# Low halves of the last down weights by VectorE, and loads that stand behind the last pair

## The chip, the cores and the metric

The kernel runs on one core of a Trainium2 chip. TensorE multiplies, VectorE and ScalarE do the element work, GpSimd does a share of it and issues some transfers, SyncE issues the others. What counts is the device time of the core in microseconds, as the median of repeated runs. Beside it there is one profiled execution, from which every view below is taken.

## The reference, cut to what matters

One inference step of a two-layer decoder on 520 rows: 512 of a prompt and 8 single decode rows, model width 1024. Layer 0 mixes tokens with windowed attention, layer 1 with gated linear attention (GLA). After the mixer each layer has a normalisation and this feed-forward part:

```python
def conv_ffn(x, buf, w_up, conv_w, conv_b, w_down):
    h = x @ w_up                                   # 1024 -> 2 x 2816
    a, u = h[..., :D_FF], h[..., D_FF:]
    ap = jnp.concatenate([buf, a], axis=1)
    c = conv_b + sum(conv_w[j] * ap[:, j:j + T] for j in range(3))
    return (gelu(c) * u) @ w_down, ap[:, T:]       # 2816 -> 1024

x = layer_norm(ALPHA * x + sublayer(x))            # after the mixer and after conv_ffn
```

All is float32. The kernel keeps that accuracy by splitting every operand into a high and a low part of the matmul type fp32r.

## The kernel before, in words

**Products.** Channels lie on partitions, rows of tokens on the free axis, in two groups: a (256 rows) and b (264). Each product of a 128x128 weight block takes three matmuls: high x high, high weight x low data, low weight x high data. A weight unit is one `128x1024` tile, 512 KB, that is eight such blocks. `product` (L219 to L241) does a whole unit for one group into one PSUM bank (`accp`); with `behind` set (L225) it does the low weight parts in a second pass (L238), not block by block (L235).

**Loading a unit** (`load_unit`, L176 to L196). SyncE fetches the raw weights into one of two buffers (`RAWS = 2`, L184), ScalarE rounds them to the high part `wh` (L189). The low part `wl` = raw - wh is made in one of two ways: by a subtraction on VectorE (L195), or by `low_by_dma` (L198 to L201), where ScalarE writes -wh into `wl` (L200) and a transfer from GpSimd's queue adds the raw weights to it from memory, on the way (L201). There are six slots of `wh`/`wl`. `load_next` starts the load of the next unit when a slot is free; `release` frees one, so a load is set off at the place in the program where a unit is finished. A scheduler then fixes the order of the instructions on each engine ahead of time; each engine works through its own queue strictly in that order. `issue_after(x)` keeps what is written inside it behind x.

**The feed-forward part.** 22 column blocks of the hidden layer. The first four go one by one, the other 18 as `ffn_pair` (L809 to L880): gate and value weights together, by seven half products of sums of blocks (a11, a12, s1 to s4, a22; L303 to L305 in `half_product`), merged by VectorE additions (`merged`, `conv`, L828), then the convolution (L860 to L863), gelu (L866), the product with the value branch (L867) and the split into high and low hidden values (`hs_a` and `hh_b` by ScalarE at L308, `hs_a` and `hl_b` by VectorE at L309). A pair takes four loads (`pair_tasks`): three "live" slots and one "half" slot. Down products of hidden blocks 0 to 13 run between the pairs (`ffn_down2`). Pairs are named here by their column block: pair 20 and pair 21 are the last two.

**The last down units.** Blocks 14 to 21 go into eight units, here d0 to d7, one per 128 output channels (`ffn_down`, L915 to L932). Four of them are begun ahead for group a (`HEADS = 4`, `down_steps`, L904 to L913) with the seven blocks that are ready before pair 21 is done: d0 and d1 with their low parts, d2 and d3 without. These four heads fill all four `accp` banks (`ACCS = 4`). After each unit and group comes a step of the normalisation (`ln_chunk`): VectorE adds the product to x (L330), which frees the bank, then squares (ScalarE, L350) and sums (L362, L363) follow; `ln_end` closes it (L366 to L441), and writes the next layer's inputs `xs_a`, `xh_b`, `xl_b` (L433 to L435). Group a runs four units ahead of group b.

**Row sums** (`row_sums`, L449 to L491) work out sums of rows of weights and inputs for the pairs' shortcut, in portions; `yield n` says after how many products the next portion may come.

The functions that the diff touches stand below with their lines.

Of the kernel before, what the change touches and what calls it, by code (L numbers as in the profile page):

```python
# [22 lines left out]
KD = 8  # L23
# [6 lines left out]
NF = 22  # L30
# [33 lines left out]
LOWS = 7  # L64
# [17 lines left out]
def parted(rows):  # L82

    return rows.rearrange("p (j t) -> p t j", t=2)


def in_turn(rows):

    return rows.rearrange("p t j -> p j t")
# [10 lines left out]
class Net:  # L100
# [70 lines left out]
    def wide(self):  # L171
        return self.acc.tile([P, 2, 512], F32, name="widep")


    def load_unit(self, u, pieces=1, late=False):
        src, nt = self.units[u][0], self.units[u][1]  # L176
        nc = self.nc
        if nt == 0:
            return self.load_rank(u)
        r = self.raw.tile([P, KD * P], F32, name="raw")  # L180
        h, l = ((self.wx if u == self.extra else self.wts).tile([P, KD * P], F32R, name=name) for name in ("wh", "wl"))
        n = nt * P // pieces
        for c in (slice(i * n, (i + 1) * n) for i in range(pieces)):
            nc.sync.dma_start(out=r[:, c], in_=src[:, c])  # L184
            if late:
                self.spawn(self.parts(u, h[:, c], l[:, c], r[:, c], src[:, c]), 1)
                continue
            if u >= HIACT:
                nc.scalar.activation(h[:, c], r[:, c], AF.Copy)  # L189
            else:  # L190
                nc.gpsimd.tensor_scalar(h[:, c], r[:, c], 1.0, 0.0, op0=ALU.mult, op1=ALU.add)
            if self.units[u][2] in (self.ffn_down2, self.ffn_down, self.ffn_gate, self.ffn_value):
                self.low_by_dma(l[:, c], h[:, c], src[:, c])
            else:
                nc.vector.tensor_tensor(l[:, c], r[:, c], h[:, c].bitcast(F32), op=ALU.subtract)  # L195
        self.w[u] = (h, l)  # L196
# [22 lines left out]
    def product(self, g, u, rh, rl):  # L219
        nc = self.nc  # L220
        h, l = self.w[u]
        nt = self.units[u][1]

        tail = u in self.phases[2::3] or g.i and u in self.phases[2:4]
        behind = g.i == 0 and nt == KD and not tail and any(e < u < e + LOWS for e in (*self.phases[2:4], *self.phases[5:6]))  # L225
        ps = self.acc.tile([P, 512], F32, name="accp")
        o = ps[:, :g.n].rearrange("p (j t) -> p j t", t=2)
        for k in range(nt):
            ks = slice(k * P, (k + 1) * P)
            xh, xl = in_turn(rh[:, k]), in_turn(rl[:, k])  # L230
            nc.tensor.matmul(o, h[:, ks], xh, start=k == 0, stop=False)  # L231
            if not tail:
                nc.tensor.matmul(o, h[:, ks], xl, start=False, stop=False)  # L233
            if not behind:
                nc.tensor.matmul(o, l[:, ks], xh, start=False, stop=not tail and k == nt - 1)  # L235
        for k in range(nt) if tail or behind else ():
            w, r = (h, rl) if tail else (l, rh)
            nc.tensor.matmul(o, w[:, k * P:(k + 1) * P], in_turn(r[:, k]), start=False, stop=k == nt - 1)  # L238
        self.final = self.nc.cur_bb.bb.instructions[-1]
        return ps[:, :g.n]  # L240
# [210 lines left out]
    def row_sums(self, i):  # L451


        nc, half, n = self.nc, KD // 2, P
        a, b = self.groups
        hi, lo = slice(half, KD), slice(0, half)
        v = nc.vector
        bias = lambda m: self.par[:, C_LNB + i * KD + m:C_LNB + i * KD + m + 1]
        step = self.pp.tile([P, half], F32, name="step")
        p0 = C_LNB + i * KD  # L460
        nc.gpsimd.tensor_tensor(step, self.par[:, p0 + half:p0 + KD], self.par[:, p0:p0 + half], op=ALU.subtract)
        wide = lambda t: t.rearrange("p (k c) -> p k c", k=half)
        even = lambda t: t.rearrange("p k (j t) -> p k t j", t=2)
        row = lambda g, k: g.x[:, k, 0:256]
        self.t1 = [self.ln.tile([P, NT - 256], F32, name=name, bufs=c)[:, :256] for name, c in (("sq", 2), ("sq", 2), ("mu", 1), ("msq", 1))]
        with self.tc.issue_after(self.rest):
            v.tensor_tensor(self.t1[0], row(a, 0), row(b, 0), op=ALU.subtract)
        for k in range(1, half):
            v.tensor_tensor(self.t1[k], row(a, k), row(b, k), op=ALU.subtract)
        yield 1  # L470
        ts = self.pp.tile([P, 2, half, NS], F32, name="tsum")
        gap = step.unsqueeze(2).broadcast_to([P, half, NS])
        for q, x, y, op in ((0, lo, hi, ALU.subtract), (1, hi, lo, ALU.add)):
            v.tensor_tensor(ts[:, q], b.x[:, x, 256:], b.x[:, y, 256:], op=ALU.subtract)
            v.tensor_tensor(ts[:, q], ts[:, q], gap, op=op)
            self.split(self.th[q][:, :, :, n:], self.tl[q][:, :, :, n:], even(ts[:, q]))
        r = wide(self.pp.tile([P, KD * P], F32, name="raw", bufs=2))
        for k in range(half):
            v.scalar_tensor_tensor(r[:, k], row(b, half + k), bias(half + k), self.t1[k], op0=ALU.add, op1=ALU.add)
        th, tl = self.th[0][:, :, :, :n], self.tl[0][:, :, :, :n]  # L480
        nc.scalar.activation(th, even(r), AF.Copy, scale=-1.0)
        for k in range(half):
            v.scalar_tensor_tensor(tl[:, k], even(r)[:, k], -1.0, th[:, k].bitcast(F32), op0=ALU.mult, op1=ALU.subtract)
        yield 2
        for k in range(half):
            v.scalar_tensor_tensor(r[:, k], r[:, k], bias(half + k), row(a, half + k), op0=ALU.subtract, op1=ALU.subtract)
        self.split(self.th[2], self.tl[2], even(r))
        yield 2
        for k in range(half):
            v.scalar_tensor_tensor(r[:, k], row(b, half + k), step[:, k:k + 1], row(b, k), op0=ALU.add, op1=ALU.subtract)  # L490
        self.split(self.th[1][:, :, :, :n], self.tl[1][:, :, :, :n], even(r))  # L491
# [316 lines left out]
    def ffn_pair(self, u, layer, j, q):  # L808


        nc, W = self.nc, self.w[u]
        a, b = self.groups
        if j == PAIRED:
            self.row_sum1()
            self.close(self.cp_cm)
            self.cp, self.cp_cm = self.open(f"merged{layer}")
            self.m = [self.cp.tile([P, 2, 2 + NT], F32, name=f"merged{i}") for i in range(2)]
            self.c = [self.cp.tile([P, 2, NT - 256], F32, name=f"conv{i}") for i in range(2)]
            for t in self.m:
                nc.gpsimd.memset(t[:, 0, 0:2], 0.0)  # L820
            self.close_psum()
            self.open_wide()
        half = KD // 2
        part = lambda g, ks: (g.xh[:, ks], g.xl[:, ks])
        lo, hi = slice(0, half), slice(half, KD)
# [5 lines left out]
        g, h = M[:, 0], M[:, 1, 2:]  # L831
# [19 lines left out]
        self.half_product(p[:, 0], W["s4"], part(b, hi), m)  # L851
        self.release()
        self.half_product(p[:, 1], W["s3"], t3, m)
        self.half -= 1
        self.load_next()
        add(M[:, :, 2 + n:], p[:, :, :m], both(C[:, 0]))
        add(h[:, :n], p[:, 1, :n], C[:, 1, :n])
        w, cb = self.taps(layer, j)
# [9 lines left out]
        self.split(a.hh[:, q], a.hl[:, q], parted(h[:, :n]))  # L868
        self.split(b.hh[:, q], b.hl[:, q], parted(h[:, n:]))
        if j == NF - 1:  # L870
            nc.scalar.dma_start(out=self.O["conv_p"][layer], in_=self.nconv_p)
            nc.scalar.dma_start(out=self.O["conv_s"][layer], in_=self.nconv_s)
            for cm in (self.cp_cm, self.pp_cm, self.fp_cm):
                self.close(cm)
            self.close_psum()
            self.open_acc()
# [420 lines left out]
            self.todo.pop(0)  # L1297
            f()

    def release(self):  # L1300
        self.live -= 1
        self.load_next()

    def run(self):
        nc = self.nc
        self.plan()
        self.nu = self.live = WSLOTS
        self.todo, self.half, self.more, self.extra = [], 0, False, None
        self.attn_open()
        self.later, self.slot, self.seq, self.norm = [], 0, 0, None  # L1310
        for i, u in self.order():
# [144 lines left out]
```

## Time and profile before

| what | value |
|---|---|
| median of three runs | 1129.21 us (1127.98 to 1132.0) |
| the profiled execution | 1128.26 us |
| span in its profile | 1126.5 us, mean granted TensorE clock 0.989 |
| TensorE busy | 1072.6 us, 95% |
| VectorE, ScalarE, GpSimd busy | 872.6, 664.6, 335.7 us |
| last down units of layer 0, of layer 1 | about 463 to 521 us, 1060 to 1113 us of the span |

The page lists busy time by engine and the costliest groups of instructions; the view of waits says, per engine and line, what the engine stood waiting for (total, times, longest); the timeline lists instructions with start, length and, in brackets, the idle time ahead of them and what ended it; a table of stretches gives busy time, granted clock (PEclk), share of the transfer engines and GB/s of each stretch.

### The profile page before, as it was taken

How to read it: one execution, taken by the hardware profiler on the slowest of the kernel's cores; microseconds unless marked ns; L12 is line 12 of the kernel's file. 1: busy time of each engine (PE TensorE's matmuls, PEld its weight loads, DVE VectorE, ACT ScalarE, POOL GpSimd, SP SyncE). 2: the span in 40 equal slices, each digit the busy share in tenths (PEclk: the TensorE clock that was granted, in tenths of full speed). 3: DMA queues.
4: the chain of work that ended last, by engine and by line, in shares of the span. 5: the costliest groups of instructions: out<-in, count | busy, mean ns of one | idle time of the engine just before them, and what ended most of it. 6: DMA issues, size and time to landing. Idle time of an engine off the chain costs nothing.

```text
span 1126.5 us, 23813 instructions
## 1 busy us (share of the span) xinstructions
PE 1072.6 (95%) x9174; PEld 1039.3 (92%) x9174; DVE 872.6 (77%) x1784; ACT 664.6 (59%) x1315; POOL 335.7 (30%) x549
## 2 busy tenths in 40 slices
PE   8999998999999999889899999999999999999985
PEld 8997798899999999889799899898899999999985
DVE  7897679888777789546967677779988778888645
ACT  5677556865666655634545555456766655565643
POOL 3576574211111111174311100374221111110263
PEclk9999999999999999999899999999999999999998
DMA  6453034677777764862134464445577777764752
GB/s 235 148 177 104 22 95 131 169 189 185 182 178 177 180 167 97 222 151 78 57 109 131 121 186 146 145 129 150 152 181 187 178 183 171 178 161 129 183 124 76
DMA packets 65616, 167.96 MB, mean 149 GB/s; under 512 B 8120, under 2 KB 28640, under 8 KB 65504
## 3 DMA queue, kind: packets, MB, share of 16 engines
q1 hardware_dynamic: 50960, 119.47, 32.9%
q0 software_dynamic: 12384, 45.09, 23.0%
q10 hardware_dynamic: 2160, 1.89, 0.5%
q8 instruction: 72, 1.18, 0.4%
q14 instruction: 40, 0.33, 0.1%
HBM read 153.76 MB, written 8.47 MB: 144 GB/s over the span
## 4 chain that ended last, share of the span: by engine, by line
PE 60%; DVE 17%; DMA 10%; ACT 6%; issue 4%; POOL 2%; SPq 0%; ACTq 0%; DVEq 0%; POOLq 0%
PE widep L303 7%; PE widep L304 7%; PE widep L305 7%; PE accp L233 5%; PE accp L231 5%; PE accp L235 5%; PE widep L895 4%; PE widep L894 4%; PE widep L896 4%; DMA raw<-in_w_down 2%; DMA wl<-in_w_down 2%; DMA vb<-dv 2%; DVE wl L195 1%; PE onep L304 1%; PE onep L303 1%
## 5 line engine op out<-in xcount | busy, mean ns | idle before, releaser
L189 ACT ACTIVATE wh<-raw 128x1024 fp32r<-128x1024 f32 (+1 forms) x92 | 96.3, 1048 | 68.4 <-PE accp L233 31.7
L308 ACT ACTIVATE wh<-raw 128x1024 fp32r<-128x1024 f32 x72 | 76.4, 1061 | 100.6 <-PE widep L895 62.9
L201 POOL DMA_DIRECT2D wl<-in_w_down x44 | 38.0, 864 | 311.8 <-ACT wl L200 307.4
L231 PE MATMUL accp<-xh_b,wh 128*128 128x264 f32 x400 | 114.3, 286 | 6.8 <-DVE hprod L804 4.6
L303 PE MATMUL widep<-th,wh 128*128 128x264 f32 (+1 forms) x432 | 119.2, 276 | 0.5 <-DVE hprod L804 0.5
L304 PE MATMUL widep<-tl,wh 128*128 128x264 f32 (+1 forms) x432 | 119.1, 276 | 0.0
L305 PE MATMUL widep<-th,wl 128*128 128x264 f32 (+1 forms) x432 | 119.1, 276 | 0.0
L235 PE MATMUL accp<-xh_b,wl 128*128 128x264 f32 x400 | 112.7, 282 | 0.0
L231 PE MATMUL accp<-xs_a,wh 128*128 128x256 f32 x400 | 109.5, 288 | 3.2 <-ACT wh L189 1.4
L233 PE MATMUL accp<-xl_b,wh 128*128 128x264 f32 x384 | 108.1, 282 | 0.0
L233 PE MATMUL accp<-xs_a,wh 128*128 128x256 f32 x384 | 104.1, 285 | 0.0
L309 DVE TENSOR_TENSOR wl<-raw,wh 128x1024 fp32r<-128x1024 f32 x72 | 87.8, 1219 | 8.8 <-ACT wh L308 8.8
L200 ACT ACTIVATE wl<-wh 128x1024 fp32r<-128x1024 f32 x86 | 90.1, 1050 | 0.9
L231 PEld LDWEIGHTS accp<-xh_b,wh 128*128 128x128 f32 x400 | 76.4, 191 | 9.1 <-DVE hprod L804 5.2
L828 DVE TENSOR_TENSOR merged<-widep,conv 128x528 f32<-128x528 f32 x72 | 37.6, 561 | 59.7 <-PE widep L305 59.6
L231 PEld LDWEIGHTS accp<-xs_a,wh 128*128 128x128 f32 x400 | 78.4, 196 | 5.2 <-ACT wh L189 1.9
L303 PEld LDWEIGHTS widep<-th,wh 128*128 128x128 f32 x432 | 82.1, 190 | 0.7 <-DVE hprod L804 0.7
L304 PEld LDWEIGHTS widep<-tl,wh 128*128 128x128 f32 x432 | 82.1, 190 | 0.0
L305 PEld LDWEIGHTS widep<-th,wl 128*128 128x128 f32 x432 | 82.1, 190 | 0.0
L303 PE MATMUL widep<-xh_b,wh 128*128 128x264 f32 x288 | 79.7, 277 | 0.6 <-POOL xh_b L500 0.6
L304 PE MATMUL widep<-xl_b,wh 128*128 128x264 f32 x288 | 79.5, 276 | 0.0
L305 PE MATMUL widep<-xh_b,wl 128*128 128x264 f32 x288 | 79.5, 276 | 0.0
(419 smaller groups left out, 4209.0 us busy)
## 6 DMA issues: line engine op xcount, KB each, us to landing
raw<-in_w_up SPq DMA_DIRECT2D x88, 512.0 KB, 3.5
raw<-in_w_down SPq DMA_DIRECT2D x44, 512.0 KB, 3.8
wl<-in_w_down POOLq DMA_DIRECT2D x44, 512.0 KB, 6.7
wl<-in_w_up POOLq DMA_DIRECT2D x42, 512.0 KB, 6.1
raw<-in_w_gla SPq DMA_DIRECT2D x24, 512.0 KB, 3.6
raw<-in_w_mix_o SPq DMA_DIRECT2D x16, 512.0 KB, 4.2
qs<-hl SPq DMA_DIRECT2D x64, 64.0 KB, 2.1
sgla<-in_state_gla SPq DMA_DIRECT2D x16, 256.0 KB, 2.8
```

Source lines behind the costliest of these rows:

```text
L189: nc.scalar.activation(h[:, c], r[:, c], AF.Copy)
L200: self.nc.scalar.activation(l, h.bitcast(F32), AF.Copy, scale=-1.0)
L231: nc.tensor.matmul(o, h[:, ks], xh, start=k == 0, stop=False)
L233: nc.tensor.matmul(o, h[:, ks], xl, start=False, stop=False)
L235: nc.tensor.matmul(o, l[:, ks], xh, start=False, stop=not tail and k == nt - 1)
L303: self.nc.tensor.matmul(o, h[:, ks], rh, start=k == 0, stop=False)
L304: self.nc.tensor.matmul(o, h[:, ks], rl, start=False, stop=False)
L305: self.final = self.nc.tensor.matmul(o, l[:, ks], rh, start=False, stop=k == KD // 2 - 1).ins
L308: self.nc.scalar.activation(hi, src, AF.Copy)
L309: self.nc.vector.tensor_tensor(lo, src, hi.bitcast(F32), op=ALU.subtract)
L894: nc.tensor.matmul(o, h[:, ks], rh, start=k == 0, stop=False)
L895: nc.tensor.matmul(o, h[:, ks], rl, start=False, stop=False)
```

## The change

Three edits.

1. Units of `ffn_down` get their low part by the subtraction on VectorE. In `product`, group a's products of these units use the low parts in the second pass.
2. While the last pair (j = NF - 1) is emitted, its four releases are collected in `held` and made at the end of its own chain: the first at once, the other three inside `issue_after` of the chain's last ScalarE instruction.
3. In `row_sums` two numbers of products between portions grow by one.

```diff
-            if self.units[u][2] in (self.ffn_down2, self.ffn_down, self.ffn_gate, self.ffn_value):
+            if self.units[u][2] in (self.ffn_down2, self.ffn_gate, self.ffn_value):
                 self.low_by_dma(l[:, c], h[:, c], src[:, c])
             else:
                 nc.vector.tensor_tensor(l[:, c], r[:, c], h[:, c].bitcast(F32), op=ALU.subtract)
...
-        behind = g.i == 0 and nt == KD and not tail and any(e < u < e + LOWS for e in (*self.phases[2:4], *self.phases[5:6]))
+        behind = self.units[u][2] == self.ffn_down and g.i == 0 or g.i == 0 and nt == KD and not tail and any(e < u < e + LOWS for e in (*self.phases[2:4], *self.phases[5:6]))
...
-        yield 1
+        yield 2
...
-        yield 2
+        yield 3
...
+        if j == NF - 1:
+            self.held = []
...
-        self.half -= 1
-        self.load_next()
+        self.release("half")
...
         if j == NF - 1:
+            kinds, self.held = self.held, None
+            done = next(x for x in reversed(nc.cur_bb.bb.instructions) if x.engine == mybir.EngineType.Activation)
+            self.release(kinds[0])
+            with self.tc.issue_after(done):
+                for kind in kinds[1:]:
+                    self.release(kind)
...
-    def release(self):
-        self.live -= 1
+    def release(self, kind="live"):
+        if self.held is not None:
+            self.held.append(kind)
+            return
+        if kind == "live":
+            self.live -= 1
+        else:
+            self.half -= 1
         self.load_next()
```

The scheduler makes a new order from it. Lines behind the first edit of `ffn_pair` are counted up to 7 further in the changed kernel (L860 is L861, L866 is L867, L828 is L830, L871 and L872 are L878 and L879). ScalarE at the end of layer 1, from the split of pair 20's hidden values to that of pair 21, before (`merged_11153` belongs to pair 20, `merged_11154` to pair 21):

```order
L871 DMA out_conv_p<-nconv_p 128x44
L308 ACTIVATE hs_a<-merged_11153 128x2x128
L308 ACTIVATE hh_b<-merged_11153 128x264
L189 ACTIVATE wh<-raw 128x1024
L872 DMA out_conv_s<-sconv 128x352
L860 ACTIVATE conv_11156<-merged_11154,par 128x512
L189 ACTIVATE wh<-raw 128x1024
L200 ACTIVATE wl<-wh 128x1024 x2
L866 ACTIVATE conv_11156<-conv_11156 128x520
L308 ACTIVATE hs_a<-merged_11154 128x2x128
L308 ACTIVATE hh_b<-merged_11154 128x264
```

And in the changed kernel (`merged_11145` is pair 20's, `merged_11146` pair 21's):

```order
L189 ACTIVATE wh<-raw 128x1024
L308 ACTIVATE hs_a<-merged_11145 128x2x128
L308 ACTIVATE hh_b<-merged_11145 128x264
L878 DMA out_conv_p<-nconv_p 128x44
L861 ACTIVATE conv_11148<-merged_11146,par 128x512
L879 DMA out_conv_s<-sconv 128x352
L867 ACTIVATE conv_11148<-conv_11148 128x520
L308 ACTIVATE hs_a<-merged_11146 128x2x128
L308 ACTIVATE hh_b<-merged_11146 128x264
L189 ACTIVATE wh<-raw 128x1024 x2
```

Two high parts of later units (d4, d5) that stood within the last pair's chain now stand behind it, their `wl` copies are gone, and the high part of d3 stands ahead of pair 20's split. VectorE at the same place, before:

```order
L828 TENSOR_TENSOR conv_11156<-widep,merged_11154 128x2x256
L828 TENSOR_TENSOR conv_11156<-widep,merged_11154 128x8
L828 TENSOR_TENSOR merged_11154<-widep,conv_11156 128x2x264
L867 SCALAR_TENSOR_TENSOR merged_11153<-conv_11155,merged_11153 128x520
L828 TENSOR_TENSOR merged_11154<-widep,conv_11156 128x256
L863 SCALAR_TENSOR_TENSOR conv_11156<-merged_11154,par,base 128x8
L309 TENSOR_TENSOR hs_a<-merged_11153,hs_a 128x2x128
L309 TENSOR_TENSOR hl_b<-merged_11153,hh_b 128x264
```

And in the changed kernel (the L195 rows are the subtractions of d2 and d3 at first, of d4 and d5 at the end):

```order
L195 TENSOR_TENSOR wl<-raw,wh 128x1024
L830 TENSOR_TENSOR conv_11148<-widep,merged_11146 128x2x256
L830 TENSOR_TENSOR conv_11148<-widep,merged_11146 128x8
L868 SCALAR_TENSOR_TENSOR merged_11145<-conv_11147,merged_11145 128x520
L195 TENSOR_TENSOR wl<-raw,wh 128x1024
L830 TENSOR_TENSOR merged_11146<-widep,conv_11148 128x2x264
L830 TENSOR_TENSOR merged_11146<-widep,conv_11148 128x256
L309 TENSOR_TENSOR hs_a<-merged_11145,hs_a 128x2x128
L309 TENSOR_TENSOR hl_b<-merged_11145,hh_b 128x264
```

And, three rows further on, the end of pair 21's chain:

```order
L868 SCALAR_TENSOR_TENSOR merged_11146<-conv_11148,merged_11146 128x520
L309 TENSOR_TENSOR hs_a<-merged_11146,hs_a 128x2x128
L309 TENSOR_TENSOR hl_b<-merged_11146,hh_b 128x264
L195 TENSOR_TENSOR wl<-raw,wh 128x1024 x2
L330 SCALAR_TENSOR_TENSOR x_a<-x_a,back,accp 128x256
```

Before, no L195 row stood here. Now pair 20's split stands behind the subtraction of d3, and the first L330 behind those of d4 and d5.

The third place is VectorE at the start of layer 1, before, from the end of group b's normalisation of layer 0 (`q_a`, `k_a` are GLA's first results of group a):

```order
L433 SCALAR_TENSOR_TENSOR x_b<-x_b,par,pv 128x264 x8
L1088 COPY ebl<-eb 128x1
L1026 SCALAR_TENSOR_TENSOR q_a<-accp,ep 128x256
L1033 TENSOR_TENSOR k_a<-accp,em 128x256
L435 SCALAR_TENSOR_TENSOR xl_b<-x_b,par,xh_b 128x264 x8
```

And in the changed kernel:

```order
L433 SCALAR_TENSOR_TENSOR x_b<-x_b,par,pv 128x264 x8
L1014 TENSOR_SCALAR dcum<-dcum,bl 128x64 x2
L1090 TENSOR_TENSOR f<-ebl,eb 128x1
L435 SCALAR_TENSOR_TENSOR xl_b<-x_b,par,xh_b 128x264 x6
L1095 COPY ebl<-eb 128x1
L435 SCALAR_TENSOR_TENSOR xl_b<-x_b,par,xh_b 128x264 x2
L1033 SCALAR_TENSOR_TENSOR q_a<-accp,ep 128x256
L1040 TENSOR_TENSOR k_a<-accp,em 128x256
```

The eight low parts of x_b have moved ahead of `q_a` and `k_a`. Edit 3 alone moves no row on any engine. In all, ScalarE loses the 16 L200 rows of these units, GpSimd their 16 transfers, and VectorE gains 16 subtractions, eight in each layer.

More of the change, by code (lines that the diff above doesn't have):

```diff
@@ L1307, in run @@
         self.nu = self.live = WSLOTS
-        self.todo, self.half, self.more, self.extra = [], 0, False, None
+        self.todo, self.half, self.more, self.extra, self.held = [], 0, False, None, None
         self.attn_open()
```

## The prediction

> **What bounds the kernel now.** I read the page first, then the waits of TensorE over the whole span.
>
> ```profile
> span 1126.5 us, 23813 instructions
> PE 1072.6 (95%) x9174; PEld 1039.3 (92%) x9174; DVE 872.6 (77%) x1784; ACT 664.6 (59%) x1315; POOL 335.7 (30%) x549
> ```
> ```profile
> PE accp L913 <- DMA wl<-in_w_down: 7.7, 6, 1.5
> PE accp L235 <- DMA wl<-in_w_down: 4.6, 4, 2.7
> PE accp L231 <- DVE hprod L804: 4.6, 3, 2.0
> PE accp L983 <- ACT xh_b L434: 3.1, 1, 3.1
> ```
>
> TensorE is the bound: 95% busy. Time can be won only where it waits, and the largest two rows wait for one thing, the transfer that completes a down unit's low part. The same view, cut to the last down units of layer 0 and of layer 1, says how much of it belongs to the change:
>
> ```profile
> PE accp L913 <- DMA wl<-in_w_down: 3.7, 3, 1.5
> PE accp L235 <- DMA wl<-in_w_down: 3.2, 2, 2.7
> PE accp L913 <- ACT hs_a L308: 1.4, 1, 1.4
> ```
> ```profile
> PE accp L913 <- DMA wl<-in_w_down: 4.0, 3, 1.5
> PE accp L235 <- DMA wl<-in_w_down: 1.4, 2, 1.2
> ```
>
> So 8.3 us in six waits in layer 0, and 5.4 us in five in layer 1. A wait costs more than its length, as TensorE's timeline shows (start, length, then the idle time in brackets), and so does the clock in a table of stretches (PEclk is the fourth entry):
>
> ```profile
> 1060.30 0.28 PE L913 MATMUL accp<-hs_a,wh 128*128 128x256 f32 x1
> 1061.51 0.38 PE L913 MATMUL accp<-hs_a,wl 128*128 128x256 f32 x1 [0.94 <-DMA wl<-in_w_down]
> 1061.72 0.39 PE L913 MATMUL accp<-hs_a,wh 128*128 128x256 f32 x2
> ...
> 1068.96 2.17 PE L913 MATMUL accp<-hs_a,wh 128*128 128x256 f32 x18
> 1070.97 0.94 PE L913 MATMUL accp<-hs_a,wl 128*128 128x256 f32 x7
> ```
> ```profile
> 485.21 0.58 PE L235 MATMUL accp<-hs_a,wl 128*128 128x256 f32 x1 [2.67 <-DMA wl<-in_w_down]
> ```
> ```profile
> 485.20:488.36 3.16, 3.15 (x15) 0.50 1.03 317
> ```
>
> Undisturbed, 18 products take 2.01 us (1068.96 to 1070.97), 0.112 each. Around the wait of 0.94 two starts lie 1.21 apart and the next two 0.21: 0.16 + 0.10 = 0.26 us lost beside the wait. After 2.67 us of idling the granted clock is 0.50, and 15 products take 3.16 us in place of 1.7: 1.5 more. Layer 0 thus loses 8.3 + 6 x 0.26 + 1.5 = 11.4 us, layer 1 5.4 + 5 x 0.26 = 6.7 us. **18.1 us is what stands to be won here.**
>
> Why are the low parts late? The queues of GpSimd and ScalarE, layer 1:
>
> ```profile
> 1061.88 0.85 POOL L201 DMA_DIRECT2D wl<-in_w_down  x1
> 1071.65 1.81 POOL L201 DMA_DIRECT2D wl<-in_w_down  x2 [8.92 <-ACT wl L200]
> ```
> ```profile
> 1065.61 1.06 ACT L189 ACTIVATE wh<-raw 128x1024 fp32r<-128x1024 f32 x1 [2.46 <-DMA raw<-in_w_down]
> 1069.35 1.06 ACT L189 ACTIVATE wh<-raw 128x1024 fp32r<-128x1024 f32 x1 [1.98 <-DMA raw<-in_w_down]
> ```
>
> ScalarE stands twice at a raw weight that hasn't landed, with the last pair's own activations queued behind; and a low part sets off only after that. Landing times of these transfers, for wl from 1050 to 1100 and then for raw from 1036 to 1080 (min, median, max):
>
> ```profile
> DMA to landing us min/median/max: 5.1/7.1/11.5
> ```
> ```profile
> DMA to landing us min/median/max: 3.4/6.4/10.4
> ```
>
> **What the change removes.** Sixteen L200 activations (16.8 us of ScalarE, at 1.05) and sixteen GpSimd transfers of 7 us each, with their second reading of 512 KB. TensorE's five waits per layer on such a transfer have no releaser left. The low part now needs wh and one subtraction, whose price I take from its twin at L309:
>
> ```profile
> L309 DVE TENSOR_TENSOR wl<-raw,wh 128x1024 fp32r<-128x1024 f32 x72 | 87.8, 1219 | 8.8 <-ACT wh L308 8.8
> L189 ACT ACTIVATE wh<-raw 128x1024 fp32r<-128x1024 f32 (+1 forms) x92 | 96.3, 1048 | 68.4 <-PE accp L233 31.7
> L828 DVE TENSOR_TENSOR merged<-widep,conv 128x528 f32<-128x528 f32 x72 | 37.6, 561 | 59.7 <-PE widep L305 59.6
> L309 DVE TENSOR_TENSOR hs_a<-merged,hs_a 128x256 fp32r<-128x256 f32 x3 | 1.3, 441 | 0.9 <-ACT hs_a L308 0.9
> ```
>
> From raw landed to low part ready: 1.05 + 1.22 = 2.3 us, against 2.1 + 0.9 + 7.1 = 10 before.
>
> **What it adds.** Eight subtractions per layer on VectorE, 9.8 us, in its queue. d0 to d7 are the eight units. I walk the changed order on layer 1's clock. Before, VectorE's queue here was:
>
> ```profile
> 1053.00 0.68 DVE L309 TENSOR_TENSOR wl<-sum,wh 128x512 fp32r<-128x512 f32 x1
> 1053.60 0.43 DVE L309 TENSOR_TENSOR hs_a<-merged,hs_a 128x256 fp32r<-128x256 f32 x1
> ...
> 1054.28 0.23 DVE L863 SCALAR_TENSOR_TENSOR conv<-merged,par,base 128x8 f32<-128x8 f32 x1
> ```
>
> With the subtractions of d0 and d1 in it, that stretch ends at 1054.5 + 2 x 1.2, or at 1056.8 with the small overlaps of neighbours. A raw buffer is free only when its subtraction is over, so raw d3 is requested at 1056.8, lands after the smallest time of the view (3.4, since no GpSimd transfer of a down unit flies beside it) at 1060.3, its high part is ready at 1061.3, its low part at 1062.5. In VectorE's queue two merging adds (0.56 each, 0.1 overlapped) and the split of pair 20's hidden values stand behind this subtraction: 1063.5, and 1063.95. TensorE, free of the pairs at 1060.3, comes to that pair's column after 18 products of the first head, at 1062.3. **A new wait of 1.6 us, 1.9 with its refill, in each layer: 3.8.** Its lower bound is 0.8 (raw d3 0.8 earlier), its upper one 3.6 (raw d3 2 us later, between its minimum 3.4 and the median 6.4).
>
> By the Trainium skill, "TensorE: Matmul & The Clock Gate", section "What's actually happening", the clock halves after an idle window of about 3.4 us. The trace has it at 0.50 after 2.67; so by the page a wait of 3.6 would cost half clock too, and one of 2.7 to 3.4 would not.
>
> Behind it I find no other wait. The remaining head products last 5.7 us, to 1069.65; the last pair's chain (convolution, two adds, gelu, product, split: 4.6 us by my walk) ends on VectorE at 1068.55, 1.1 ahead, because neither late raw stands in its way now: its four releases come after it. d4 and d5 are requested when the buffers of d2 and d3 are free (1060.0, 1062.5), lie there by 1066, and are split between 1068.5 and 1071.75; the fifth product wants d4's high part at 1073.0. The low parts, used last in group a, are wanted 1.8 us later still. d6 and d7 come out at 1080.6 and 1085.9, ahead of their products. The 1.4 us for hs_a in layer 0 goes with the raw waits ahead of it.
>
> **The first bank** is the thing to watch: accumulators number four, all taken by the heads, and the step that frees one (L330) stands behind the subtractions of d4 and d5 (1071.75, then 0.48): 0.8 us to spare.
>
> **VectorE beside GpSimd.** GpSimd's x minus mean, six steps, once alone and once beside VectorE's weight subtractions (busy us is the second number):
>
> ```profile
> 1105.70:1110.20 4.50, 4.36 (x6) 1.00 0.00 0
> 534.20:541.40 7.20, 6.84 (x6) 1.00 0.51 164
> ```
>
> GpSimd gets slower beside VectorE, by up to 1.6. In the down stage two subtractions per layer (d6, d7) fall among its steps, and no wait of TensorE there names GpSimd: I take nothing, at most 2.4 us a layer. By the Trainium skill, "SBUF — State Buffer", section "SBUF: two separate sides", a VectorE instruction with two SBUF inputs and a GpSimd one that reads SBUF lock each other out for a whole instruction; the rows agree in sign. Were all of it on the path, the time by that page would be 1111 + 4.8, about 1116.
>
> **Between the layers** group b's normalisation holds TensorE. Its last product, its last L330, what that leads to, the wait, and the granted clock (0.50) behind it:
>
> ```profile
> 520.92 0.28 PE L235 MATMUL accp<-hh_b,wl 128*128 128x264 f32 x1
> ```
> ```profile
> 526.02 0.48 DVE L330 SCALAR_TENSOR_TENSOR x_b<-x_b,back,accp 128x264 f32<-128x264 f32 x1
> ...
> 542.28 3.28 DVE L433 SCALAR_TENSOR_TENSOR x_b<-x_b,par,pv 128x264 f32<-128x264 f32 x8
> ```
> ```profile
> 543.52 3.55 PE L983 MATMUL accp<-xh_b,wh 128*128 128x264 f32 x8 [3.08 <-ACT xh_b L434]
> ```
> ```profile
> 543.52:547.00 3.48, 3.48 (x9) 0.50 0.00 0
> ```
>
> The last product ends at 521.2, but L330 starts 4.8 us later, behind group a's work. The changed order ends group a's normalisation one product earlier, so more of it lies under group b's products and L330 can follow its product at once. From L330 to L433 it was 16.3 us (526.02 to 542.28); so xh_b comes some 16.3 us after the last product. TensorE's own work in between filled 543.52 - 3.08 - 521.2 = 19.2 us, some 2.4 of it small waits for group a that the same shift removes, so it stands at the door after 16.8: the 3.1 us go. But the low parts of x_b now precede q_a and k_a in VectorE's queue (8 steps in 3.3 us), which can hand up to 3.3 back, and against that stand the 2.4 of group a. I take **+3**, the long wait alone; bounds -2 (the wait only moves, and the half clock behind it, the last row, costs 2 more) and +5 (3.1 and most of 2.4).
>
> **The end** of layer 1: the last product at 1112.76, the step that takes it 1.2 us later.
>
> ```profile
> 1112.76 0.28 PE L235 MATMUL accp<-hh_b,wl 128*128 128x264 f32 x1
> ```
> ```profile
> 1113.97 0.48 DVE L330 SCALAR_TENSOR_TENSOR x_b<-x_b,back,accp 128x264 f32<-128x264 f32 x1
> ```
>
> Of the 0.9 us between (1113.04 to 1113.97) the earlier end of group a may save some: +0.6, bounds 0 and 0.9.
>
> **The sums of rows.** In the changed order every row of every engine is the same with and without the two new numbers. Nothing.
>
> **Sum.** 18.1 - 3.8 + 3 + 0.6 = 17.9. The profiled execution took 1128.3 us (span 1126.5, 1.8 around it), 0.9 under the median 1129.2 of the runs: 1128.3 - 17.9 = 1110.4, on the median **1111**. With the terms' bounds, 1105 to 1118 (new waits 2 x 0.8 earlier and GLA +5: 1107, less 2 for what I may have undercounted of refills; GLA at -2 and 1 us more a layer: 1118). Chance 0.73.
>
> **Rivals.**
> First, the new wait is larger: raw d3 lands in 5.4 us, the wait is 3.6 + 0.26, and the clock halves (1.5, row at 485.20). That is 5.4 instead of 1.9 in each layer, 7.0 in all; with nothing won between the layers 1111 + 7 + 3 = 1121. For it: the median landing of 6.4. Against it: that median was taken while wl transfers flew. Chance 0.13.
> Second, no change: raws still take 10.4, as the longest here, because pairs and other units fill the queues. The wait is 8.6 + 1.8 a layer; d5, requested and landing late both, then holds L330 and a bank 1.4 us more. 2 x 11.8 = 23.6 against 21.7 won: 1131. Chance 0.06.
> Third, **slower**: the same queue from 10.8 us of landing on, since VectorE now stands at the raw with the bank's release behind it, where GpSimd stood alone. At 11.5, the longest landing of the wl view, each layer loses 11.5 + 2.6, 28 in all: 1129.2 + 28 - 21.7 = 1135. For it: VectorE's queue is in order and d3 is ahead of everything. Against it: sixteen transfers fewer. Chance 0.06.
> Fourth, the row sums do what they are called: up to the 4.6 us at hprod, 1106. The unchanged order speaks against it. Chance 0.02.
>
> **The numbers.** This kernel's runs tell about 0.3% (3.4 us) from no change. Faster: 0.73 + 0.13 + 0.02 = 0.88; same 0.06; slower 0.06. The range takes the first rival in, down to 1104: 1104 to 1121.
>
> **What would show it.** Right: no wait on wl<-in_w_down at the lines of the last units; one wait of 1 to 2 us per layer in the first head, put down to VectorE's hs_a; ScalarE without idling on raw before the last pair's conv; a granted clock of 1.00 throughout layer 0's down stage; the 3.1 us for xh_b gone; hprod's 4.6 unchanged. Wrong: a wait at L330's banks, raw landings above 6 us after the pairs, q_a or k_a waited for by TensorE.

## The result, and the profile after

The changed kernel takes 1111.48 us (median of four runs, 1108.69 to 1115.32) against 1128.60 (four runs, 1127.08 to 1132.0): a ratio of 0.9847, 95% interval 0.9808 to 0.9885. The interval lies wholly below 1. Forecast were 1111 us, 1104 to 1121. (Ratios here and below come with the runs and are not quite the quotients of the medians.)

The page of the changed kernel (span, then busy time by engine):

```profile
span 1110.4 us, 23783 instructions
PE 1065.9 (96%) x9174; PEld 1033.9 (93%) x9174; DVE 892.7 (80%) x1800; ACT 650.3 (59%) x1299; POOL 330.3 (30%) x533
```

VectorE has 16 instructions and 20 us more, ScalarE and GpSimd 16 less each. What TensorE waited for in the last down units, first layer 0 and then layer 1 (the rows that answer to the three and the two before):

```profile
PE accp L920 <- DVE merged L830: 1.4, 1, 1.4
```
```profile
PE accp L920 <- DVE hs_a L309: 1.4, 1, 1.4
```

Eleven waits of 13.7 us in all have become two of 2.8. None is for a transfer. The waits of the whole program:

```profile
PE accp L231 <- DVE hprod L804: 4.9, 4, 2.0
PE widep L303 <- DVE hprod L804: 2.9, 2, 1.5
...
PE accp L231 <- ACT v_a L1057: 1.9, 1, 1.9
...
PE accp L990 <- ACT v_a L1057: 1.0, 1, 1.0
```

The first row for hprod is as before (4.9 against 4.6 us), the second is not: at L303 it was 0.5 us, and is now 2.9. One of its two waits is new. It stands in layer 1, in the first pair:

```profile
PE widep L303 <- DVE hprod L804: 1.4, 1, 1.4
```

It shows (1.3 to 2.3 us long) in all seven profiles of kernels that have the subtractions and the changed kernel's order at this place, and in none of the three that have the transfers; before, TensorE waited 0.6 us there for another value. VectorE's rows stand in the same order there before and after; why TensorE needs a later one of them now is not shown. The wait of 3.1 us for xh_b at the start of GLA is gone, and two for v_a stand there now.

To see where the time went I cut each profile at four places of TensorE's timeline: the starts of the first head product and of the last group b product of each layer's last down units. The pieces, in us:

| kernel | up to the heads of layer 0 | last down units, layer 0 | between | last down units, layer 1 | end | span |
|---|---|---|---|---|---|---|
| before | 464.8 | 56.1 | 539.3 | 52.6 | 13.8 | 1126.5 |
| changed | 466.8 | 46.4 | 537.6 | 47.2 | 12.4 | 1110.4 |
| difference | +2.0 | -9.7 | -1.7 | -5.3 | -1.4 | -16.1 |

The first piece has the same order in both kernels up to its last 8 us, and on TensorE throughout. Over all twelve profiles of this study it lies between 462.3 and 467.4: its 2.0 us are scatter from run to run. The 1.7 us of "between" are two effects, 2.5 won in GLA and 0.8 lost in the pairs; the part on the prediction comes back to them.

### The profile page after: what moved, and what is told of

Read it like the earlier page. It is cut to its first block, busy times and chain, and to the rows that moved or that the text cites. A ratio compares the mean times of both kernels' runs of the same rounds, so it can differ in the third digit from the quotient of the medians.

```text
span 1110.4 us, 23783 instructions
## 1 busy us (share of the span) xinstructions
PE 1065.9 (96%) x9174; PEld 1033.9 (93%) x9174; DVE 892.7 (80%) x1800; ACT 650.3 (59%) x1299; POOL 330.3 (30%) x533
## 4 chain that ended last, share of the span: by engine, by line
PE 64%; DVE 19%; DMA 7%; ACT 4%; issue 4%; POOL 1%; SPq 0%; DVEq 0%; ACTq 0%; POOLq 0%
PE widep L303 7%; PE widep L305 7%; PE widep L304 7%; PE accp L233 6%; PE accp L231 6%; PE accp L235 5%; PE widep L901 5%; PE widep L903 5%; PE widep L902 5%; DMA vb<-dv 2%; DMA raw<-in_w_up 2%; PE accp L920 2%; DVE xs_a L435 1%; PE onep L305 1%; PE onep L304 1%
## 5 line engine op out<-in xcount | busy, mean ns | idle before, releaser
L303 PE MATMUL widep<-th,wh 128*128 128x264 f32 (+1 forms) x432 | 119.3, 276 | 2.9 <-DVE hprod L804 2.9
L231 PE MATMUL accp<-xh_b,wh 128*128 128x264 f32 x400 | 113.9, 285 | 7.7 <-DVE hprod L804 4.9
L231 PE MATMUL accp<-xs_a,wh 128*128 128x256 f32 x400 | 108.0, 285 | 5.2 <-ACT v_a L1057 1.9
L201 POOL DMA_DIRECT2D wl<-in_w_down x28 | 24.2, 863 | 283.9 <-ACT wl L200 283.4
L233 PE MATMUL accp<-xs_a,wh 128*128 128x256 f32 x384 | 102.5, 281 | 0.4 <-DVE xs_a L309 0.3
L195 DVE TENSOR_TENSOR wl<-raw,wh 128x1024 fp32r<-128x1024 f32 (+2 forms) x64 | 79.3, 1246 | 9.8 <-ACT wh L189 9.0
L231 PEld LDWEIGHTS accp<-xh_b,wh 128*128 128x128 f32 x400 | 75.8, 189 | 10.3 <-DVE hprod L804 5.7
L303 PEld LDWEIGHTS widep<-th,wh 128*128 128x128 f32 x432 | 82.1, 190 | 3.3 <-DVE hprod L804 1.7
L830 DVE TENSOR_TENSOR merged<-widep,conv 128x528 f32<-128x528 f32 x72 | 37.3, 559 | 58.9 <-PE widep L305 58.9
L231 PEld LDWEIGHTS accp<-xs_a,wh 128*128 128x128 f32 x400 | 77.0, 193 | 7.4 <-ACT v_a L1057 2.1
L303 PE MATMUL widep<-xh_b,wh 128*128 128x264 f32 x288 | 79.6, 276 | 0.0
```

The source lines that it names most:

```text
L303: self.nc.tensor.matmul(o, h[:, ks], rh, start=k == 0, stop=False)
```

## The experiments

**1. Which edit carries it.** Theory A: the late transfers are the cause, so edit 1a alone (low parts by subtraction) brings nearly everything. Theory B: the releases are, since raw weights hold ScalarE up inside the last pair's chain. Edit 1a alone:

```diff
-            if self.units[u][2] in (self.ffn_down2, self.ffn_down, self.ffn_gate, self.ffn_value):
+            if self.units[u][2] in (self.ffn_down2, self.ffn_gate, self.ffn_value):
```

> Edit 1a alone: the last down units' low parts by subtraction on VectorE, still used block by block, releases as before. Theory A (the late transfers that complete the low parts are the cause): the five waits per layer on wl<-in_w_down are gone and nearly all of the gain is here, 1111 to 1116 us; what is left over to the changed kernel is 1 to 4 us, because d4's and d5's weights still stand inside the last pair's chain. Theory B (the releases are the cause: ScalarE stands at raw weights inside the last pair's chain): at most a third of the gain, 1123 or more.

Measured: 1111.73 us, ratio 0.9823 (0.9781 to 0.9865). Layer 0's and layer 1's pieces are 47.5 and 47.9 us. Its waits there, layer 0 and then layer 1:

```profile
PE accp L913 <- DVE merged L828: 1.6, 1, 1.6
PE accp L913 <- ACT hs_a L308: 0.4, 2, 0.3
```
```profile
PE accp L913 <- DVE hs_a L309: 1.5, 1, 1.5
```

This is the changed kernel's picture without the second pass (edit 1b) and without edit 2. Theory A holds. For the other two edits 1 to 4 us were expected; the pieces show 1.1 and 0.7, which can't be told from nothing by the times.

With the second pass in group a as well (edits 1a and 1b):

```diff
-        behind = g.i == 0 and nt == KD and not tail and any(...)
+        behind = self.units[u][2] == self.ffn_down and g.i == 0 or g.i == 0 and nt == KD and not tail and any(...)
```

> Edits 1a and 1b: low parts by subtraction on VectorE and used in a second pass by group a; releases as before. Theory A: 1111 to 1116, within 2 us of edit 1a alone, since a subtraction is ready 2.3 us after its raw weights and the second pass gives only 1.8 us of grace to units that are hardly late. Rival: the second pass is what hides the low parts, and this is 4 us or more faster than edit 1a alone.

Measured: 1111.54 us, 0.9826 (0.9789 to 0.9863), the same. Lows used last hide nothing here, because a subtraction's result isn't late.

Edit 2 alone (the four releases collected in `held` and made behind the chain, low parts still by transfer):

> Edit 2 alone: the last pair's four releases behind its own chain, low parts still by transfer. Theory A: ScalarE no longer idles at raw weights inside the chain and the wait for hs_a in layer 0 (1.4 us) goes, but the waits on wl<-in_w_down stay or grow, since the transfers of d4 and d5 are asked for no earlier: 1124 to 1130. Theory B: 1112 to 1120.

Measured: 1132.53 beside 1132.29, ratio 1.0006 (0.9984 to 1.0028): nothing won. Theory B falls. On this chip "nothing" is above the 1124 to 1130 I had named. TensorE's waits in the last down units, layer 0 and layer 1:

```profile
PE accp L231 <- DVE x_a L330: 3.5, 2, 3.2
PE accp L920 <- DMA wl<-in_w_down: 2.3, 2, 1.9
PE accp L235 <- DMA wl<-in_w_down: 0.8, 1, 0.8
```
```profile
PE accp L920 <- DMA wl<-in_w_down: 4.9, 2, 4.5
PE accp L235 <- DMA wl<-in_w_down: 2.0, 2, 1.7
```

The wait for hs_a in layer 0 is gone, as expected of a chain that no raw weight holds up; the waits for transfers stay, the longest has grown to 4.5 us, and a new one of 3.2 us for a bank (L330) has come. Freed of one wait, TensorE runs into the next.

Edit 3 alone:

```diff
-        yield 1
+        yield 2
...
-        yield 2
+        yield 3
```

> Edit 3 alone: the two numbers of products between portions of the row sums grow by one. The order on every engine is that of the kernel before, so every theory but one expects 1128.6 within 2 us and the 4.6 us of TensorE's waits for hprod unchanged within 1 us; the theory that the sums of rows spread over more products would give 1124 to 1126.

Measured: 1129.99 beside 1132.29, ratio 0.9998 (0.997 to 1.0026). The waits for hprod at L231 come to 4.9 us in its profile, against 4.6 before. The third edit does nothing that these runs can tell.

**2. The new wait in the first head.** In the changed kernel VectorE's timeline of layer 1, and TensorE's first product behind the wait:

```profile
1051.31 0.69 DVE L868 SCALAR_TENSOR_TENSOR merged<-conv,merged 128x520 f32<-128x520 f32 x1
1052.01 1.23 DVE L195 TENSOR_TENSOR wl<-raw,wh 128x1024 fp32r<-128x1024 f32 x1
1053.16 1.03 DVE L830 TENSOR_TENSOR merged<-widep,conv 128x528 f32<-128x528 f32 x2
1054.11 0.41 DVE L309 TENSOR_TENSOR hs_a<-merged,hs_a 128x256 fp32r<-128x256 f32 x1
```
```profile
1054.57 0.38 PE L920 MATMUL accp<-hs_a,wh 128*128 128x256 f32 x1 [1.43 <-DVE hs_a L309]
```

Pair 20's product is done at 1052.0; its split follows at 1054.1, behind d3's subtraction and two adds. d3's low part isn't wanted until the end of its head. In layer 0 the first product behind the wait is another one:

```profile
470.25 0.42 DVE L309 TENSOR_TENSOR hs_a<-merged,hs_a 128x256 fp32r<-128x256 f32 x1
```
```profile
470.48 0.62 PE L920 MATMUL accp<-hs_a,wh 128*128 128x256 f32 x3 [1.35 <-DVE merged L830]
```

It starts before the split ends (470.67), so it does not need the split; it waits for the two adds, which end at 470.33. They read `widep`, and `ffn_pair` ends by closing that PSUM pool and opening the heads' one, so it is the bank of the next head that fits. The split ends 0.3 us later, so both hold the head by about the same, and both stand behind d3's subtraction. So the subtraction was put elsewhere (L195, and one line in `ffn_pair` behind the splits). First behind the last pair's whole chain:

```diff
-                nc.vector.tensor_tensor(l[:, c], r[:, c], h[:, c].bitcast(F32), op=ALU.subtract)
+                d3 = self.units[u][2] == self.ffn_down and self.units[u][3][2] == 3
+                with self.tc.issue_after(self.split20) if d3 else ExitStack():
+                    nc.vector.tensor_tensor(l[:, c], r[:, c], h[:, c].bitcast(F32), op=ALU.subtract)
...
+        if j >= NF - 2:
+            self.split20 = nc.cur_bb.bb.instructions[-1]
```

> The changed kernel once more, beside the variants of this call. Every theory: 0.985 of the kernel before, within 0.004.

> The changed kernel with one thing different: d3's low-part subtraction is put behind the last pair's own chain on VectorE, so pair 20's split no longer stands behind it. d3's low part is wanted only at the end of its head, about 9 us later. Theory (the new wait of 1.4 us per layer in the first head is VectorE's queue, not the arithmetic of pair 20): the wait falls to 0.3 us or less in both layers, since the split then follows two adds only, and 1.1 to 1.4 us per layer are won: 2 to 3 us less than the changed kernel, the down stages 1.0 to 1.4 us shorter each. Rival (ScalarE's half of the split, behind d3's high part, sets it): the wait stays at 1 us or more and the time is the same within 1 us.

Measured: the changed kernel 1113.27 us, 0.9829 (0.9794 to 0.9864); this variant 1112.32, 0.9824 (0.9795 to 0.9853). The wait in the first head is gone, as the theory said, and the rival (ScalarE's half) falls. But the time is the same, not 2 to 3 us less, and the pieces are no shorter: 49.2 and 47.9 us, against 48.6 and 47.2 beside it. Waits in the variant's last down units, layer 0 and layer 1, and ScalarE in layer 1:

```profile
PE accp L233 <- DVE x_a L332: 2.4, 1, 2.4
```
```profile
PE accp L233 <- DVE x_a L332: 1.8, 1, 1.8
```
```profile
1060.19 1.06 ACT L189 ACTIVATE wh<-raw 128x1024 fp32r<-128x1024 f32 x1 [4.22 <-DMA raw<-in_w_down]
```

d5 can't be fetched until d3's subtraction has freed the raw buffer. Counted from the first head product the subtraction starts 6.5 us later than in the changed kernel (7.6 against 1.1), and that makes d5 late; d5's subtraction stands in VectorE's queue ahead of the L330 (here L332) that frees the next bank, and TensorE waits there. The gain was turned into a new wait. VectorE's order differs in one more place, at the first pair of layer 1: one hprod row stands further ahead (2.5 us sooner, counted from the pair's first product), and the new wait for hprod is absent.

A third variant put the last pair's two merging adds behind pair 20's split as well:

```diff
+        with self.tc.issue_after(self.split20) if j == NF - 1 else ExitStack():
+            add(M[:, :, 2 + n:], p[:, :, :m], both(C[:, 0]))
+            add(h[:, :n], p[:, 1, :n], C[:, 1, :n])
```

> As the variant with d3's subtraction behind the last pair's chain, and that pair's last two merging adds behind pair 20's split too. Theory: no wait for pair 20's hidden values at all, but the last pair's chain ends 0.8 us later than in the other variant, so 0.5 us of a new wait for the last pair's hidden values: 1 to 2.5 us less than the changed kernel. If the wait in layer 0, which the trace puts down to a merging add, is for a PSUM bank that these adds free, then it stays or grows in layer 0 alone and this variant wins nothing there.

Measured: 1122.18 us, 0.9902 (0.9876 to 0.9929), 9 us slower than the changed kernel, a miss. Its waits, of the whole program:

```profile
PE sc L338 <- DVE x_a L332: 4.4, 1, 4.4
PE accp L233 <- DVE x_a L332: 2.7, 1, 2.7
...
PE accp L925 <- DVE merged L832: 1.8, 2, 0.9
```

The heads now wait 0.9 us for the adds in each layer, so the adds do free something that they need. The two longer waits are those of the first variant, since raw d5 is late here too. ScalarE in layer 1:

```profile
1069.26 1.06 ACT L189 ACTIVATE wh<-raw 128x1024 fp32r<-128x1024 f32 x1 [4.40 <-DMA raw<-in_w_down]
```

In layer 1 the first L332 now stands behind d5's subtraction as well, so TensorE waits 4.4 us already at the first one. The pieces are 51.3 and 53.0 us.

**3. What a late raw weight costs.** The prediction's rivals priced a late raw weight one for one, through VectorE's queue and the first bank. To make one late with nearly the same order (one row of VectorE differs, in layer 0), d5 was fetched three times into the same buffer:

```diff
+            if self.units[u][2] == self.ffn_down and self.units[u][3][2] == 5:
+                for _ in range(2):
+                    nc.sync.dma_start(out=r[:, c], in_=src[:, c])
```

> The changed kernel with the raw weights of d5 fetched three times into the same buffer, one after the other, so that they land about 7 us later (64 instead of 57 on layer 1's clock). The order is that of the changed kernel but for one place: in layer 1 the first L330, which frees the first bank, stands behind d5's subtraction, in layer 0 it stands ahead of it. Theory (a late raw weight is paid for one by one through VectorE's queue and the bank): in layer 1 TensorE waits 3.5 to 4.5 us for a bank, and half clock follows, the down stage is 4 to 6 us longer than in the changed kernel; in layer 0 nothing or under 1 us. Rival (the transfers themselves delay the others, or d5's weights are wanted at once): both layers lose alike.

Measured: 1122.86 us, 0.9906 (0.9872 to 0.9941). VectorE and TensorE in layer 1:

```profile
1064.96 1.23 DVE L198 TENSOR_TENSOR wl<-raw,wh 128x1024 fp32r<-128x1024 f32 x1 [0.49 <-ACT wh L192]
1070.62 1.23 DVE L198 TENSOR_TENSOR wl<-raw,wh 128x1024 fp32r<-128x1024 f32 x1 [4.43 <-ACT wh L192]
1071.76 0.47 DVE L333 SCALAR_TENSOR_TENSOR x_a<-x_a,back,accp 128x256 f32<-128x256 f32 x1
```
```profile
1072.29 0.70 PE L339 MATMUL sc<-x_a,ones_a 128*128 128x256 f32 x2 [4.11 <-DVE x_a L333]
```

VectorE stands 4.43 us at d5, L333 behind it, and TensorE waits 4.11 us: 3.5 to 4.5 were expected. (The product that waits is the sum over x_a, L339; it needs what L333 writes, and the first product into the bank that L333 frees follows 0.35 us behind.) The piece is 53.4 us against 47.2, 6.2 longer (the wait, its refill, and half clock after it). In layer 0 I had expected less than 1 us and found this wait:

```profile
PE accp L234 <- DVE x_a L333: 2.9, 1, 2.9
```

There the first L333 is ahead of d5's subtraction, but the second stands behind it, and holds the next bank: 2.9 us of waiting, though VectorE stood 4.8 us. The mechanism is seen in both layers, the price of one for one in layer 1 only, and my expectation for layer 0 had looked at one bank only. The layers lose unlike amounts, about 3 and 6 us, which speaks against the rival.

**4. The place between.** If the split may not stand behind d3's subtraction, and d5's buffer not be freed late, the subtraction belongs right behind the split. The edit is that of the first variant with `j == NF - 2` in its last condition.

> The changed kernel with d3's low-part subtraction behind pair 20's split only, ahead of the last pair's convolution. Theory (two things share VectorE's queue: pair 20's split, which the first head waits for, and the subtraction that frees d5's raw buffer): the wait for pair 20's hidden values falls to 0.3 us or less as when the subtraction stood behind the whole chain, but raw d5 is asked for 4 to 5 us earlier than there, so no wait of 1.8 to 2.4 us for a bank takes its place: the down stages come to 45 to 46 us (layer 0) and 45.5 to 46.2 us (layer 1), 1 to 1.5 us less than the changed kernel each, the time 0.979 to 0.982 of the kernel before. Rival (the time saved at the split is always paid again at the bank): a bank wait of over 1 us, stages as in the changed kernel, 0.983 to 0.985.

> The changed kernel, beside the variant of this call: 0.983 to 0.985 of the kernel before, waits of 1.3 to 1.6 us in the first head of each layer.

Measured on one chip: 1107.57 us (1105.67 to 1109.07), 0.9806 (0.9778 to 0.9835), and for the changed kernel 1111.04 (1109.13 to 1116.44), 0.9849 (0.9812 to 0.9886). The two ranges of six runs don't touch, the intervals of the ratios to before just overlap. The waits of the variant, layer 0 and layer 1:

```profile
PE sc L338 <- DVE x_a L332: 0.5, 1, 0.5
PE accp L924 <- ACT hs_a L310: 0.3, 1, 0.3
```
```profile
PE sc L338 <- DVE x_a L332: 0.5, 1, 0.5
```

The wait for pair 20 is gone but for 0.3 us, and half a microsecond comes back at the first L332, since the last pair's chain is now behind the subtraction. The pieces are 46.2 and 46.5 us, where the changed kernel beside it had 46.2 and 47.2. Expected were 45 to 46 and 45.5 to 46.2: the ratio came out in its range, the pieces did not, and layer 0 won nothing. So only 0.7 us of the 3.5 between the medians are seen in the place that was changed. Another 1.4 are seen elsewhere: at the first pair of layer 1 the scheduler made another order of VectorE's rows, as in the first variant, the last two hprod rows come 1.6 and 1.9 us sooner, and the wait for hprod there (1.4 us in the changed kernel beside it) is absent. This variant is the fastest seen, but it differs in two places, and the rest of its margin is not accounted for.

## Why the prediction was right, point by point

**What stood to be won.** 11.4 and 6.7 us of losses in the two layers, less 1.9 of a new wait each, made 9.5 and 4.8; the pieces shrank by 9.7 and 5.3 us. That the transfers were the cause, and not the chain behind ScalarE's waits, is shown by edits 1a and 2 run alone. Edit 1a takes away two things at once, the low part's own flight and its traffic beside the raw loads (whose landing times fall, below); no run tells them apart.

**The new wait.** Predicted 1.6 us in each layer, measured 1.4 and 1.4 (1.2 to 1.5 in three profiles of the changed kernel), in the place named: the first head. In layer 1 it is for pair 20's values, as said; in layer 0 it is for the two merging adds, which stand in the same queue behind d3's subtraction. Raw d3 landed as the sum assumed. The landing times of raw weights from 1036 to 1080 in the changed kernel (min, median, max), against 3.4, 6.4 and 10.4 before:

```profile
DMA to landing us min/median/max: 3.4/3.4/4.8
```

That settles the first three rivals: they all needed late raw weights. Their price of one for one was met in layer 1, 4.1 us of waiting for 4.4 us of standing when d5 was made late; in layer 0 it was 2.9 for 4.8.

**ScalarE's idling.** I had written that ScalarE would no longer idle on raw weights ahead of the last pair's convolution. It still does, 3.7 us in two waits before that point. It costs nothing that the trace shows: the gelu and the split behind them start within 0.1 us of the VectorE results that they need (1049.41 for 1049.35, 1052.03 for 1052.00).

**Between the layers** is the step that failed in its path: +3 was taken, "the 3.1 us go". They did go at xh_b, but two waits of 2.9 us in all replaced them. ScalarE and TensorE in the changed kernel:

```profile
526.78 1.06 ACT L211 ACTIVATE wh<-raw 128x1024 fp32r<-128x1024 f32 x1 [2.58 <-DMA raw<-in_w_gla]
...
529.43 0.36 ACT L1057 COPY v_a<-accp 128x256 f32<-128x256 f32 x1
```
```profile
529.84 0.38 PE L231 MATMUL accp<-xs_a,wh 128*128 128x256 f32 x1 [1.94 <-ACT v_a L1057]
...
533.83 3.00 PE L990 MATMUL accp<-xh_b,wh 128*128 128x264 f32 x8 [1.05 <-ACT v_a L1057]
536.63 3.04 PE L990 MATMUL accp<-xl_b,wh 128*128 128x264 f32 x8
539.74 1.22 PE L1048 MATMUL sc<-q_a,k_a 128*128 128x128 f32 x4
```

The copy that empties a bank stands behind a raw GLA weight and group b's normalisation on ScalarE; and xl_b, now ahead of q_a and k_a, paces TensorE, as feared. From layer 0's last product to the first q_a x k_a product it is 26.0 us before (520.9 to 546.9) and 26.5 after (513.2 to 539.7). But that mark is not the same work: the changed kernel has eight xl_b products ahead of it. Up to the first product that takes GLA's output (`accp<-hs_a`) it is 186.1 us before and 183.6 after; the three profiles with transfers lie at 186.1 to 187.1, the nine with subtractions at 182.7 to 185.8. So about 2.5 us were won after all. What went are small waits for group a's xs_a (0.9 us before), which the prediction had set against the low parts of x_b, and most of one wait that it did not mention, 0.2 us after:

```profile
PE tp L1061 <- DVE sg L1181: 1.8, 1, 1.8
```

Why sg comes sooner is not shown. That the size is near the 3 of the sum is luck: the 3.1 us that were to give it were paid again.

**The end** gave 1.4 us, not 0.6, above the bound of 0.9 that I set. The profile shows both halves, the last product and the step that takes it:

```profile
1098.09 0.28 PE L235 MATMUL accp<-hh_b,wl 128*128 128x264 f32 x1
...
1098.40 0.49 DVE L330 SCALAR_TENSOR_TENSOR x_b<-x_b,back,accp 128x264 f32<-128x264 f32 x1 [1.23 <-PE accp L235]
```

L330 starts as the product ends (1098.37), so the whole 0.9 was won, and the chain from there to the end is 12.0 us against 12.6. Every kernel with subtractions has this, 12.3 to 12.6 us for its end against 13.8. I had bounded only the gap, not the work behind it.

**The sums of rows**: nothing from edit 3, as the unchanged order said. But "hprod's 4.6 unchanged" holds only of the row at L231: edit 1a brought the new wait at L303, and the stretch from the first pair to the heads of layer 1 is 0.8 us longer (246.6 against 245.7). The sum had no term for it.

So of the 17.9 us forecast, the 14.9 for the down units and the end came as 16.4, and the 3 between the layers as 1.7, 2.5 won by another path less 0.8 lost in the pairs. In this pair of profiles 2.0 of scatter go off again: 16.1 us by the spans, 17.1 by the medians. The terms of the down units were right in mechanism and size; that the total fits to half a microsecond is luck.

## What to carry to other kernels

Before a wait is priced, look at what is queued behind the instruction that ends it. Here one subtraction of 1.2 us decided over three things at once: the split queued behind it, the buffer that it frees for a later load, and the accumulator that the next instruction in the queue frees. Standing too early it cost a wait of 1.2 to 1.5 us in each layer, too late one of 1.8 to 2.4, and in the place between one of 0.5.

A part of a change that leaves every engine's order as it was can be struck from the sum before anything runs; here edit 3 was such a part. The other way round, compare the whole order before a variant is read as one change: two variants of one subtraction had another order 250 us ahead of it, and a wait of 1.4 us less there.

## What the runs showed of the hardware that I had not expected

How long TensorE waited does not say whether its clock halves afterwards. The table of stretches right behind a wait (the fourth entry is the granted clock), for a wait of 1.53 us in the changed kernel's second profile, and for 1.56 us at the same place with edit 1a alone:

```profile
471.70:475.40 3.70, 3.67 (x21) 0.63 0.81 262
```
```profile
470.30:473.50 3.20, 3.20 (x28) 1.00 0.62 216
```

In the last down units half clock followed waits of, among others, 1.53, 1.59, 2.43, 2.67 and 4.11 us, and none followed 1.56, 1.81, 2.37 and 2.91. The plainest case stands near 205 us, where every kernel has the same order and TensorE waits 1.94 to 1.99 us for hprod: half clock followed in 4 of the 12 profiles, and not in the other 8. The 4 us behind that wait, before and in the changed kernel:

```profile
204.10:208.10 4.00, 4.00 (x22) 0.63 1.03 193
```
```profile
206.30:210.30 4.00, 3.73 (x30) 1.00 1.03 186
```

With the 1.53 us it set in only 1.1 us after TensorE had resumed (1.53 us of waiting end at 471.73, products lie 0.21 apart from 472.82 on). This made most of the difference that layer 0's piece was 48.6 us in one profile of the changed kernel and 46.2 and 46.4 in two others. By the Trainium skill, "TensorE: Matmul & The Clock Gate", section "What's actually happening", activity is judged in a free-running window of 3.4 us, which fits a clock that depends on where a wait falls; its rule that an idle window of that length is needed does not fit 1.53 us. In the prediction I charged 1.5 us for half clock to any wait above 2.7: it is a chance, and half clock has been seen from 1.53 us on.
